# Feed-forward: a second buffer for the activations and a later place for half of the units' sums and splits; mixer: the convolution norm's two sums later

## The chip, the cores and the metric

The kernel runs on one core of one Trainium2 chip. The metric is device time in microseconds (us), the median of several executions; one further execution was profiled. The core's engines work side by side, each through its own queue in order, and meet through semaphores: TensorE (PE in the profile) multiplies matrices into PSUM, VectorE (DVE) and ScalarE (ACT) compute on tiles in PSUM and SBUF, GpSimd (POOL) computes on tiles in SBUF, SyncE (SP) issues most DMAs.

## The reference

Two transformer layers and one RWKV-7 layer over 512 tokens of width 1024, all in float32. The change touches the feed-forward, which occurs three times, and the convolution branch of the RWKV layer:

```
def _sq_relu_mlp(x, w_up, w_down):
    return jnp.square(jax.nn.relu(x @ w_up)) @ w_down      # 1024 -> 4096 -> 1024
...
x = _layer_norm(DN_ALPHA * x + _sq_relu_mlp(x, w_up[i], w_down[i]), ln2_g[i], ln2_b[i])   # layers 0 and 1
...
x = x + jnp.square(jax.nn.relu(h2 @ w_ff1[l])) @ w_ff2[l]                                # RWKV layer
...
def _conformer_conv_mixer(glu_in, conv_w, conv_b, ln_g, ln_b):
    u = glu_in[..., :D_CONV] * jax.nn.sigmoid(glu_in[..., D_CONV:])
    u = causal depthwise convolution of u (31 taps) + conv_b
    u = _layernorm(u, ln_g, ln_b)
    return jax.nn.silu(u)
```

## The kernel before

**Products.** Each float32 operand is split into a rounded part (hi) and the remainder (lo), and a product is three matrix products: hi x hi, hi x lo, lo x hi (`mm3`, lines 290 to 292). A split of a tile in SBUF (`split_sb`, lines 388 and 389) is a copy on ScalarE that makes hi and a subtraction on VectorE or GpSimd that makes lo. Weights come by DMA into `wraw` and are split into `whi` and `wlo`: those of an up unit by `load_w` (lines 265 to 273), those of a down in `down`. There are 6 whi and 6 wlo buffers.

**Feed-forward (`ffn`).** The 4096 hidden features are handled as 16 up units of 256 features. `up(i)` multiplies the weights of a unit with all 512 tokens into two psm tiles (there are two psm buffers; unit 0 uses psa), and ScalarE applies Relu (line 440) and Square (line 441) into the tile `hf`. Two consecutive up units form one of 8 down units. A down is a matrix product of 2 x 2 blocks (token halves and feature halves) done with seven block products instead of eight, so it needs sums and differences of blocks of the activations and of the weights. Those of the activations are the combinations in lines 448 to 451 on VectorE, which write the blocks 3 to 6 of `hf`; the blocks 0 to 2 and then 3 to 6 are split into `hh` and `hl`. Those of the weights are in lines 488 to 493 on GpSimd. The products of a down go into psa tiles, of which there are four, two for each block product, and VectorE adds each to the output x (line 460; line 458 the first time) or to a running sum q (line 505); then the psa tile is free.

The order of issue is up(0), up(1), and then for each down unit u but the last: up(2u + 2), down(u), up(2u + 3). On each engine instructions run in the order of a schedule that was made when the program was built: the order of issue gives the priority, and an instruction that is not ready in the planned time lets others pass. So TensorE's period is: two up units, one down. The first two up units' products are followed by unit 2's, which needs a psm tile back from unit 1's Relu. The buffers of `hh` and `hl` are three deep, `hf` has one.

**Mixer.** In the RWKV layer `second_mixer` works through 8 chunks of 128 features in a software pipeline of stages; in each stage `interleave` mixes several generators: projections, the inverse and the chunk recurrence of earlier chunks, the convolution and the gates. Each generator yields the cost of what it has just issued, has a planned total, and the one with the smallest fraction done is advanced; at a tie the one that stands first in the list. The sums of the convolution's layer norm are one such generator, in stage 7:

```
interleave(*late, *work[::-1], (n, branches(i)))
...
def mean(self):
    ps = self.g.ps("psd")
    self.g.nc.tensor.matmul(ps, self.g.ones, self.sum, start=True, stop=True)
```

`mean` sums over features with a product by ones in a psd tile; `center(j)` loads a chunk, subtracts the mean on GpSimd, stores it, squares it on ScalarE and adds the square on GpSimd to `cnsq`; `var` is a second product by ones in a psd tile, followed by a root on ScalarE and a reciprocal on VectorE. `norm(j)` normalises chunk j in stage 8 and writes it over the rows of H that the gates read; `project` multiplies the result. psd has one buffer; the gates (`branch_gate`, 24 products and a Tanh in line 1318) use it too, two of them in stage 7 and four in stage 8.

Of the kernel before, what the change touches and what calls it, by code (L numbers as in the profile page):

```python
# [11 lines left out]
F32 = mybir.dt.float32  # L12
# [276 lines left out]
def mm3(nc, ps, w, x, first, last):  # L289
    nc.tensor.matmul(ps, w[0], x[0], start=first, stop=False)  # L290
    nc.tensor.matmul(ps, w[0], x[1], start=False, stop=False)  # L291
    nc.tensor.matmul(ps, w[1], x[0], start=False, stop=last)  # L292


def proj_fm(g, W, X, m0, tag="psm"):

    ps = g.ps(tag)
    n = len(W)
    for kc in range(n):
        w = tuple(a[:, m0:m0 + 128] for a in W[kc])  # L300
        mm3(g.nc, ps, w, (X[0][:, kc, :], X[1][:, kc, :]), kc == 0, kc == n - 1)
    return ps
# [84 lines left out]
def split_sb(g, src, hi, lo, eng=None):  # L387
    g.nc.scalar.activation(hi, src, AF.Copy)  # L388
    (eng or g.nc.gpsimd).tensor_tensor(lo, src, hi.bitcast(F32), op=ALU.subtract)  # L389
# [13 lines left out]
def ffn(g, w_up, w_down, X, alpha, hp, tmp, late, norm, fm=None, fill=None):  # L403
# [15 lines left out]
    def first_two(W):  # L419

        pss = [g.ps("psa") for _ in range(2)]
        for half, t in enumerate(HALF_TOKENS):
            for e, ps in enumerate(pss):
                for kc in range(8):
                    w = tuple(a[:, e * 128:e * 128 + 128] for a in W[kc])
                    mm3(nc, ps[:, t], w, (X[0][:, kc, t], X[1][:, kc, t]), kc == 0, kc == 7)
                if half == 0:
                    late[e]()
        return pss

    def up(i):

        plain = i // 2 == units - 1
        W = g.load_w(w_up[:, i * 256:i * 256 + 256], eng=nc.gpsimd if i > 1 else None)
        F = tmp.tile([128, 8, 256], F32, name="hf", tag="hf")
        pss = first_two(W) if i == 0 else None
        for e in range(2):
            p3 = (pss[e] if pss else proj_fm(g, W, X, e * 128)).rearrange("p (a t) -> p a t", a=2)
            o = F[:, 1:3, :] if e else F[:, 0:8:7, :]
            nc.scalar.activation(o, p3, AF.Relu)  # L440
            nc.scalar.activation(o, o, AF.Square)
        hh = hp.tile([128, 7, 256], F32R, name="hh", tag="hh")
        hl = hp.tile([128, 7, 256], F32R, name="hl", tag="hl")
        split_sb(g, F[:, 0:3, :], hh[:, 0:3, :], hl[:, 0:3, :], V)
        if plain:
            split_sb(g, F[:, 7, :], hh[:, 3, :], hl[:, 3, :], V)
        else:
            V.tensor_tensor(F[:, 3, :], F[:, 7, :], F[:, 2, :], op=ALU.add)
            V.tensor_tensor(F[:, 4, :], F[:, 3, :], F[:, 0, :], op=ALU.subtract)
            V.tensor_tensor(F[:, 5, :], F[:, 0, :], F[:, 7, :], op=ALU.subtract)  # L450
            V.tensor_tensor(F[:, 6, :], F[:, 1, :], F[:, 4, :], op=ALU.subtract)  # L451
            split_sb(g, F[:, 3:7, :], hh[:, 3:7, :], hl[:, 3:7, :], V)
        h.append((hh, hl))

    def add(tb, c, ps):
        xs = g.x[tb][:, c * 512:c * 512 + 512]
        if (tb, c) not in seen and alpha != 1.0:
            V.scalar_tensor_tensor(xs, xs, alpha, ps, op0=ALU.mult, op1=ALU.add)
        else:
            V.tensor_tensor(xs, ps, xs, op=ALU.add)  # L460
        seen.add((tb, c))

    def down(u):
        q = w_down[u * 512:u * 512 + 512, :].rearrange("(j e p) n -> e p j n", e=2, p=128)
        new = lambda: g.wraw.tile([128, 1024], F32, name="wraw", tag="wraw")

        def quarter(e, c):
            t = new()
            nc.sync.dma_start(t.rearrange("p (j n) -> p j n", j=2), q[e][:, :, c * 512:c * 512 + 512])
            return t  # L470

        def parts(t, eng=None):
            hi = g.whi.tile([128, 1024], F32R, name="whi", tag="whi")
            lo = g.wlo.tile([128, 1024], F32R, name="wlo", tag="wlo")
            split_sb(g, t, hi, lo, eng)
            return hi, lo

        def product(W, k, ps, first=True, last=True):
            for t in range(2):
                for j in range(2):  # L480
                    x = tuple(a[:, k, t * 128:t * 128 + 128] for a in h[2 * u + j])
                    w = tuple(a[:, j * 512:j * 512 + 512] for a in W)
                    mm3(nc, ps[t], x, w, first and j == 0, last and j == 1)

        b11, b21, b12, b22 = quarter(0, 0), quarter(1, 0), quarter(0, 1), quarter(1, 1)
        B11, B21 = parts(b11), parts(b21)
        t3 = new()
        nc.gpsimd.tensor_tensor(t3, b22, b12, op=ALU.subtract)
        nc.gpsimd.tensor_tensor(b12, b12, b11, op=ALU.subtract)
        nc.gpsimd.tensor_tensor(b11, b22, b12, op=ALU.subtract)  # L490
        T2, T1, T3 = parts(b11), parts(b12, V), parts(t3, V)
        B22 = parts(b22, V)
        nc.gpsimd.tensor_tensor(b21, b21, b11, op=ALU.subtract)
        T4 = parts(b21)

        for k, W in ((1, B11), (2, B21), (6, T2), (5, T1), (7, T3), (3, B22), (4, T4)):
            ps = Q1 if k == 1 else [g.ps("psa") for _ in range(2)]
            product(W, BLOCK[k], ps, k > 1 or u == 0, k > 1 or u == units - 2)
            for t in range(2):
                if k in QS:  # L500
                    q = QS[k][:, t, :]
                    if u == 0:
                        nc.scalar.copy(q, ps[t])
                    else:
                        V.tensor_tensor(q, q, ps[t], op=ALU.add)
                elif k > 1:
                    add(2 * (k == 4) + t, int(k == 3), ps[t])

    def combine(ts):

        for t in ts:
            q5, q6, q7 = (QS[k][:, t, :] for k in (5, 6, 7))
            add(t, 0, Q1[t])
            V.tensor_tensor(q6, q6, Q1[t], op=ALU.add)
            V.tensor_tensor(q7, q7, q6, op=ALU.add)
            V.tensor_tensor(q6, q6, q5, op=ALU.add)
            V.tensor_tensor(q5, q5, q7, op=ALU.add)
            add(t, 1, q6)
            add(2 + t, 0, q7)
            add(2 + t, 1, q5)  # L520

    def down_last(u):
        for c in range(2):
            W = g.load_w(w_down[u * 512:u * 512 + 512, c * 512:c * 512 + 512], eng=nc.gpsimd)
            for tb in range(4):
                ps = g.ps("psa")
                for kc in range(4):
                    k = (kc % 2, 3 - kc % 2)[tb // 2]
                    x = tuple(a[:, k, tb % 2 * 128:tb % 2 * 128 + 128] for a in h[2 * u + kc // 2])
                    mm3(nc, ps, x, W[kc], kc == 0, kc == 3)  # L530
                add(tb, c, ps)
                if (c, tb) == (0, 1):
                    combine((1,))
                if c == 1:
                    norm(tb)
                    if fm and tb > 1:
                        fm(tb - 2)

    up(0)
    up(1)  # L540
    for u in range(units - 1):
        up(2 * u + 2)
        down(u)
        if u == units - 2:
            combine((0,))
        up(2 * u + 3)
    down_last(units - 1)
    if fill:
        fill()
# [575 lines left out]
def second_mixer(g, outer):  # L1125
    nc, tc, d = g.nc, g.tc, g.d
    H = g.X
    with ExitStack() as st:
# [25 lines left out]
        with ExitStack() as s2, ExitStack() as s3, ExitStack() as s4:  # L1154
# [22 lines left out]
            outs = iter(range(8))  # L1177

            def sums():
                yield 0.0  # L1180
                cn.mean()
                yield 4.0
                for j in range(8):
                    cn.center(j, ka)
                    yield 1.0
                cn.var()

            def conv_out(n):
# [52 lines left out]
            for i in range(1, 9):  # L1241
                n = 6.0 * CONVS[i] + 4.0 * GATES[i] + (i == 8) * (8.0 + 4.0 * OUTS[0])
                work = [(16.0, wkv_proj(g, i, parts[i], env))] if i < 8 else []
                work += [(4.0, wkv_inputs(g, i - 1, parts[i - 1], env))]
                late = [(10.0, wkv_inverse(g, i - 2, parts[i - 2], env))] if i > 1 else []
                late += [(17.0, wkv_chunks(g, i - 3, parts[i - 3], env))] if i > 2 else []
                if i == SUMS:
                    work += [(12.7, sums())]
                interleave(*late, *work[::-1], (n, branches(i)))
            s4.close()  # L1250
            cn.pool = g.pool(s4, "wkc", 4, side="right")
# [16 lines left out]
            for m in range(8):  # L1268
                t, u = cn.tile(), cn.tile()
# [488 lines left out]
```

## Time and profile before

| | us |
|---|---|
| median of 3 runs | 2481.47 (2478.55 to 2486.14) |
| profiled execution | 2481.95 |
| its span in the profile | 2479.8 |
| TensorE busy | 2364.9 |

The span runs from the first to the last instruction; the rest of the profiled execution's time lies around it. A time in the profile is a start in us from the span's start. Busy time of TensorE counts matrix products, whose ends are modelled; two starts are a better measure of pace than one duration.

### The profile page before, as it was taken

To read this page: it belongs to the slowest core of one execution; us is meant where nothing else is said; L and a number is where in the kernel's file an instruction comes from. 1 tells how busy PE (TensorE), PEld (TensorE's weight loads), DVE (VectorE), ACT (ScalarE), POOL (GpSimd) and SP (SyncE) were. 2 spreads that over 40 slices of the span, in tenths; PEclk is the share of its full clock that TensorE was granted. 3 is DMA by queue.
4 is the path that set the end of the run, shared out by engine and by line. 5 is a ranking of instruction groups with operands and counts; after the bars stand their busy time and mean duration, and the time that the engine had idled before them with its cause. 6 is when DMAs were issued, how large, how long until landed. Compare 5 with 4: busy or idle time off the path is not lost.

```text
span 2479.8 us, 36415 instructions
## 1 busy us (share of the span) xinstructions
PE 2364.9 (95%) x14140; PEld 1898.6 (77%) x14140; DVE 1481.9 (60%) x2782; ACT 1283.0 (52%) x2005; POOL 1030.6 (42%) x571
## 2 busy tenths in 40 slices
PE   8999999999999999999999999999988999899998
PEld 6779778787777787877777877777766679787786
DVE  3776565666443655564685587877756542645556
ACT  5774454445465645444455454666655533544443
POOL 1114677662111025767632232323253114476772
PEclk9999999999999999999999999999998999999999
DMA  7445232347565244232372576666664468232322
GB/s 209 94 141 166 85 116 71 115 121 172 140 136 117 62 124 121 71 119 86 103 202 85 118 167 146 147 144 150 134 173 119 124 172 248 77 102 85 119 81 73
DMA packets 302349, 312.19 MB, mean 126 GB/s; under 512 B 61280, under 2 KB 234976, under 8 KB 302048
## 3 DMA queue, kind: packets, MB, share of 16 engines
q1 hardware_dynamic: 280432, 239.60, 31.9%
q0 software_dynamic: 21168, 68.17, 15.2%
q8 instruction: 111, 1.82, 0.3%
q10 hardware_dynamic: 576, 2.10, 0.2%
q14 instruction: 62, 0.51, 0.1%
HBM read 221.47 MB, written 20.19 MB: 97 GB/s over the span
## 4 chain that ended last, share of the span: by engine, by line
PE 55%; POOL 13%; issue 11%; DVE 9%; DMA 6%; ACT 6%; SPq 0%; POOLq 0%; DVEq 0%; ACTq 0%
PE psm L290 7%; PE psm L291 7%; PE psm L292 7%; POOL wlo L389 4%; PE psa L290 4%; PE psa L291 4%; PE psa L292 4%; POOL wlo L273 3%; DMA wlo<-wraw 2%; PE pst L1416 2%; PE psd L290 2%; PE pss L292 2%; PE pss L291 2%; PE pss L290 2%; PE psd L292 2%
## 5 line engine op out<-in xcount | busy, mean ns | idle before, releaser
L290 PE MATMUL psm<-xT,whi 128*128 128x512 f32 (+1 forms) x1192 | 476.2, 400 | 23.3 <-ACT hf L440 12.3
L292 PE MATMUL psm<-xT,wlo 128*128 128x512 f32 (+1 forms) x1192 | 469.7, 394 | 5.4 <-DMA wlo<-wraw 5.4
L291 PE MATMUL psm<-xT,whi 128*128 128x512 f32 (+1 forms) x1192 | 471.0, 395 | 0.5 <-DVE xT L352 0.5
L267 ACT ACTIVATE whi<-wraw 128x1024 fp32r<-128x1024 f32 (+3 forms) x287 | 285.7, 1005 | 290.8 <-PE psa L292 101.5
L271 POOL DMA_DIRECT2D wlo<-wraw x147 | 127.3, 872 | 729.0 <-ACT wlo L270 497.4
L273 POOL TENSOR_TENSOR wlo<-wraw,whi 128x1024 fp32r<-128x1024 f32 x122 | 315.5, 2620 | 102.0 <-ACT whi L267 73.4
L389 POOL TENSOR_TENSOR wlo<-wraw,whi 128x1024 fp32r<-128x1024 f32 x84 | 212.9, 2534 | 241.9 <-ACT whi L388 241.9
L290 PEld LDWEIGHTS psm<-xT,whi 128*128 128x128 f32 x1192 | 226.7, 190 | 74.7 <-ACT hf L440 13.6
L292 PEld LDWEIGHTS psm<-xT,wlo 128*128 128x128 f32 x1192 | 226.6, 190 | 53.1 <-DMA wlo<-wraw 6.5
L291 PEld LDWEIGHTS psm<-xT,whi 128*128 128x128 f32 x1192 | 227.4, 191 | 44.6 <-DVE xT L352 0.9
L290 PE MATMUL psa<-whi,hh 128*128 128x512 f32 x600 | 239.0, 398 | 15.6 <-DVE x L460 15.5
L291 PE MATMUL psa<-wlo,hh 128*128 128x512 f32 x600 | 236.6, 395 | 0.0
L292 PE MATMUL psa<-whi,hl 128*128 128x512 f32 x600 | 236.4, 395 | 0.0
L388 ACT ACTIVATE whi<-wraw 128x1024 fp32r<-128x1024 f32 x147 | 151.7, 1053 | 123.9 <-PE psa L292 61.8
L1407 DVE SCALAR_TENSOR_TENSOR psc<-glu,cw,psc 128x512 f32<-128x512 f32 x232 | 173.8, 749 | 5.9 <-ACT psc L1403 2.2
L388 ACT ACTIVATE hh<-hf 128x768 fp32r<-128x768 f32 (+1 forms) x96 | 87.8, 914 | 145.2 <-DVE hf L451 143.4
L389 DVE TENSOR_TENSOR hl<-hf,hh 128x768 fp32r<-128x768 f32 (+1 forms) x96 | 124.3, 1295 | 60.2 <-ACT hh L388 60.2
L290 PEld LDWEIGHTS psa<-whi,hh 128*128 128x128 f32 x600 | 112.8, 188 | 49.7 <-DVE x L460 23.1
L389 DVE TENSOR_TENSOR wlo<-wraw,whi 128x1024 fp32r<-128x1024 f32 x63 | 86.4, 1396 | 92.5 <-ACT whi L388 87.8
L270 ACT ACTIVATE wlo<-whi 128x1024 fp32r<-128x1024 f32 (+3 forms) x147 | 140.1, 956 | 2.3 <-PE psm L292 0.7
L292 PEld LDWEIGHTS psa<-whi,hl 128*128 128x128 f32 x600 | 112.8, 188 | 27.2 <-DVE hl L389 0.7
L291 PEld LDWEIGHTS psa<-wlo,hh 128*128 128x128 f32 x600 | 112.8, 188 | 25.8
(464 smaller groups left out, 5208.6 us busy)
## 6 DMA issues: line engine op xcount, KB each, us to landing
wlo<-wraw POOLq DMA_DIRECT2D x123, 512.0 KB, 5.3
wraw<-in_w_up SPq DMA_DIRECT2D x64, 512.0 KB, 4.5
wraw<-in_w_down SPq DMA_DIRECT2D x64, 512.0 KB, 3.6
wraw<-in_w_ff SPq DMA_DIRECT2D x64, 512.0 KB, 3.8
wraw<-in_w_in SPq DMA_DIRECT2D x56, 512.0 KB, 4.9
wraw<-in_od_w_in SPq DMA_DIRECT2D x24, 512.0 KB, 4.3
wraw<-in_ple_w_gate SPq DMA_DIRECT2D x16, 512.0 KB, 4.6
brow<-in_rows SPq DMA_DIRECT2D x13, 512.0 KB, 6.7
```

Source lines behind the costliest of these rows:

```text
L267: nc.scalar.activation(hi[:, :m], raw[:, :m], AF.Copy)
L270: nc.scalar.activation(lo[:, :m], hi[:, :m].bitcast(F32), AF.Copy, scale=-1.0)
L271: nc.gpsimd.dma_start(lo[:, :m].bitcast(F32), raw[:, :m], accum_op=ALU.add)
L273: eng.tensor_tensor(lo[:, :m], raw[:, :m], hi[:, :m].bitcast(F32), op=ALU.subtract)
L290: nc.tensor.matmul(ps, w[0], x[0], start=first, stop=False)
L291: nc.tensor.matmul(ps, w[0], x[1], start=False, stop=False)
L292: nc.tensor.matmul(ps, w[1], x[0], start=False, stop=last)
L388: g.nc.scalar.activation(hi, src, AF.Copy)
L389: (eng or g.nc.gpsimd).tensor_tensor(lo, src, hi.bitcast(F32), op=ALU.subtract)
L1407: nc.vector.scalar_tensor_tensor(acc if j == 30 else part, u[:, j:j + 512], cw[:, fc * 31 + j:fc * 31 + j + 1], part, op0=ALU.mult, op1=AL ...
L1416: nc.tensor.matmul(ps[o], lhs[o], rhs[o], start=start, stop=stop)
```

## The change

In the feed-forward `hf` gets a second buffer, and `up` ends behind Relu and Square; what it did with `hf` after that (combinations and splits) becomes the function `blocks`, which `up` returns with its arguments bound. For units 0, 1 and 2u + 3 it is called at once, as before; for the units 2u + 2 it is called behind down(u). In the mixer the generator `sums` yields 2 parts instead of 0 ahead of the mean and 3 further parts ahead of the variance, and its planned total goes from 12.7 to 17.5.

```
--- before.py
+++ after.py
@@ -432,13 +432,16 @@
 
         plain = i // 2 == units - 1
         W = g.load_w(w_up[:, i * 256:i * 256 + 256], eng=nc.gpsimd if i > 1 else None)
-        F = tmp.tile([128, 8, 256], F32, name="hf", tag="hf")
+        F = tmp.tile([128, 8, 256], F32, name="hf", tag="hf", bufs=2)
         pss = first_two(W) if i == 0 else None
         for e in range(2):
             p3 = (pss[e] if pss else proj_fm(g, W, X, e * 128)).rearrange("p (a t) -> p a t", a=2)
             o = F[:, 1:3, :] if e else F[:, 0:8:7, :]
             nc.scalar.activation(o, p3, AF.Relu)
             nc.scalar.activation(o, o, AF.Square)
+        return functools.partial(blocks, F, plain)
+
+    def blocks(F, plain):
         hh = hp.tile([128, 7, 256], F32R, name="hh", tag="hh")
         hl = hp.tile([128, 7, 256], F32R, name="hl", tag="hl")
         split_sb(g, F[:, 0:3, :], hh[:, 0:3, :], hl[:, 0:3, :], V)
@@ -536,14 +539,16 @@
                     if fm and tb > 1:
                         fm(tb - 2)
 
-    up(0)
-    up(1)
+    up(0)()
+    up(1)()
     for u in range(units - 1):
-        up(2 * u + 2)
+
+        later = up(2 * u + 2)
         down(u)
+        later()
         if u == units - 2:
             combine((0,))
-        up(2 * u + 3)
+        up(2 * u + 3)()
     down_last(units - 1)
     if fill:
         fill()
@@ -1177,12 +1182,13 @@
             outs = iter(range(8))
 
             def sums():
-                yield 0.0
+                yield 2.0
                 cn.mean()
                 yield 4.0
                 for j in range(8):
                     cn.center(j, ka)
                     yield 1.0
+                yield 3.0
                 cn.var()
 
             def conv_out(n):
@@ -1245,7 +1251,7 @@
                 late = [(10.0, wkv_inverse(g, i - 2, parts[i - 2], env))] if i > 1 else []
                 late += [(17.0, wkv_chunks(g, i - 3, parts[i - 3], env))] if i > 2 else []
                 if i == SUMS:
-                    work += [(12.7, sums())]
+                    work += [(17.5, sums())]
                 interleave(*late, *work[::-1], (n, branches(i)))
             s4.close()
             cn.pool = g.pool(s4, "wkc", 4, side="right")
```

## Rows read from the trace of the kernel before

**Rows 1.** The page: busy time, share of the span and instructions of each engine.
```profile
PE 2364.9 (95%) x14140; PEld 1898.6 (77%) x14140; DVE 1481.9 (60%) x2782; ACT 1283.0 (52%) x2005; POOL 1030.6 (42%) x571
```

**Rows 2.** Who waited for whom: us in total, times, longest us.
```profile
PE psa L290 <- DVE x L460: 15.5, 14, 1.7
PE psm L290 <- ACT hf L440: 12.3, 3, 4.7
...
PE psq L1661 <- DVE s L1655: 4.3, 3, 2.7
PE psd L1368 <- POOL cnsq L1363: 4.1, 1, 4.1
...
PE psd L1350 <- POOL cnsum L1345: 1.8, 1, 1.8
...
ACT hf L440 <- DVE hl L389: 27.3, 20, 1.6
```

**Rows 3.** Timeline of TensorE, feed-forward: start us, us, instruction, [idle before <-releaser].
```profile
361.64 0.39 PE L292 MATMUL psa<-whi,hl 128*128 128x512 f32 x1
363.18 0.50 PE L290 MATMUL psa<-whi,hh 128*128 128x512 f32 x1 [1.14 <-DVE x L460]
363.51 0.39 PE L291 MATMUL psa<-wlo,hh 128*128 128x512 f32 x1
...
449.39 0.50 PE L290 MATMUL psa<-whi,hh 128*128 128x512 f32 x1 [1.69 <-DVE x L460]
```

**Rows 4.** Timeline of VectorE, the same period.
```profile
357.08 0.42 DVE L448 TENSOR_TENSOR hf<-hf 128x256 f32<-128x256 f32 x1
...
360.30 2.22 DVE L389 TENSOR_TENSOR hl<-hf,hh 128x1024 fp32r<-128x1024 f32 x1 [0.53 <-ACT hh L388]
362.44 0.68 DVE L460 TENSOR_TENSOR x<-psa,x 128x512 f32<-128x512 f32 x1
...
369.06 0.69 DVE L460 TENSOR_TENSOR x<-psa,x 128x512 f32<-128x512 f32 x1 [0.70 <-PE psa L292]
```

**Rows 5.** Timeline of ScalarE, the same period.
```profile
350.14 1.06 ACT L388 ACTIVATE hh<-hf 128x1024 fp32r<-128x1024 f32 x1 [5.69 <-DVE hf L451]
352.56 0.60 ACT L440 ACTIVATE hf<-psm 128x512 f32<-128x512 f32 x1 [1.35 <-DVE hl L389]
...
359.20 1.06 ACT L388 ACTIVATE hh<-hf 128x1024 fp32r<-128x1024 f32 x1 [0.51 <-DVE hf L451]
```

**Rows 6.** Timeline of GpSimd, the same period.
```profile
358.77 2.66 POOL L389 TENSOR_TENSOR wlo<-wraw,whi 128x1024 fp32r<-128x1024 f32 x1 [10.15 <-ACT whi L388]
361.40 10.47 POOL L273 TENSOR_TENSOR wlo<-wraw,whi 128x1024 fp32r<-128x1024 f32 x4
```

**Rows 7.** Instructions on the tile hf: ns of one, minimum/median/maximum.
```profile
L389 DVE TENSOR_TENSOR hl<-hf,hh x96: 416/959/3159, 247.0 to 2450.8; 128x768 fp32r<-128x768 f32 x48, 128x1024 fp32r<-128x1024 f32 x42, 128x256 fp32r<-128x256 f32 x6
...
L448 DVE TENSOR_TENSOR hf<-hf x42: 410/847/2632, 243.2 to 2408.9; 128x256 f32<-128x256 f32 x42
```

**Rows 8.** Timeline of ScalarE at the first entry of a feed-forward.
```profile
252.66 1.06 ACT L388 ACTIVATE hh<-hf 128x1024 fp32r<-128x1024 f32 x1 [8.57 <-DVE hf L451]
255.07 0.60 ACT L440 ACTIVATE hf<-psm 128x512 f32<-128x512 f32 x1 [1.35 <-DVE hl L389]
```

**Rows 9.** Windows behind two entries: stretch, us, TensorE busy (products), granted clock, DMA.
```profile
255.70:259.40 3.70, 3.68 (x9) 0.54 0.02 4
...
2148.70:2154.00 5.30, 5.21 (x13) 0.53 0.03 6
```

**Rows 10.** Timeline of the mixer: the two sums; a gate's Tanh, first and last of six.
```profile
1803.69 1.12 PE L1350 MATMUL psd<-cnsum,ca 128*128 128x512 f32 x2 [1.81 <-POOL cnsum L1345]
...
1860.96 2.07 PE L1368 MATMUL psd<-cnsq,ca 128*128 128x512 f32 x2 [4.10 <-POOL cnsq L1363]
...
1833.14 0.69 ACT L1318 ACTIVATE bgt<-psd,half 128x512 f32<-128x512 f32 x1
...
1922.73 0.69 ACT L1318 ACTIVATE bgt<-psd,half 128x512 f32<-128x512 f32 x1
```

More of the change, by code (lines that the diff above doesn't have):

```diff
@@ L434, in up @@
         W = g.load_w(w_up[:, i * 256:i * 256 + 256], eng=nc.gpsimd if i > 1 else None)
-        F = tmp.tile([128, 8, 256], F32, name="hf", tag="hf")
+        F = tmp.tile([128, 8, 256], F32, name="hf", tag="hf", bufs=2)
         pss = first_two(W) if i == 0 else None
@@ L441, in up, with blocks @@
             nc.scalar.activation(o, o, AF.Square)
+        return functools.partial(blocks, F, plain)
+    def blocks(F, plain):
         hh = hp.tile([128, 7, 256], F32R, name="hh", tag="hh")
@@ L537, in down_last @@
                         fm(tb - 2)
-    up(0)
-    up(1)
+    up(0)()
+    up(1)()
     for u in range(units - 1):
-        up(2 * u + 2)
+        later = up(2 * u + 2)
         down(u)
+        later()
         if u == units - 2:
             combine((0,))
-        up(2 * u + 3)
+        up(2 * u + 3)()
     down_last(units - 1)
@@ L1179, in sums @@
             def sums():
-                yield 0.0
+                yield 2.0
                 cn.mean()
@@ L1185, in sums @@
                     yield 1.0
+                yield 3.0
                 cn.var()
@@ L1247, in second_mixer @@
                 if i == SUMS:
-                    work += [(12.7, sums())]
+                    work += [(17.5, sums())]
                 interleave(*late, *work[::-1], (n, branches(i)))
```

## The prediction

> **What bounds the kernel now.** I read the page first: TensorE is busy 95% of the span [rows 1]. So a change can only win what TensorE idles, 115 us in all, or make it idle more. Next the list of who waited for whom, which says which of these idle times the change touches. Four entries do [rows 2]: TensorE waits 15.5 us in 14 places for an accumulation that frees a psa buffer (L460), 12.3 us in 3 places for a Relu that frees a psm buffer (L440), and 4.1 us and 1.8 us once each for the mixer's two sums. Together 33.7 us, 1.4% of the time. Then the timeline of one feed-forward period, engine by engine, for the reason of the first entry; the entry of a feed-forward for the second; the mixer's timeline for the last two.
>
> The wait at 363.18 recurs two periods later at 449.39, so a period (two up units of 48 products each, one down of 84) takes 43 us [rows 3]. Until 361.64 products start 0.23 us apart; the next starts 1.54 us later, and the one after that 0.33 us later. So an idle time of 1.14 us costs 1.31 + 0.10 = 1.41 us. It waits for the accumulation at 362.44, whose products had ended well before: VectorE was in the 2.22 us split of the unit's last four blocks, which began at 360.30 [rows 4]. Follow that split back: it needs the copy hh at 359.20 on ScalarE, this the combinations from 357.08 on, these the unit's Relu, which started at 352.56 [rows 4, 5]. And that Relu had waited 1.35 us for "DVE hl L389": not for its products, but until the unit before had been read out of the only hf buffer. This wait stands 20 times in the list, 27.3 us in all [rows 2]. So a late Relu makes a late split, a late split a late accumulation, and this the idle TensorE.
>
> **The change, part by part.**
>
> *The second hf buffer.* It costs no instruction. The Relu at 352.56 no longer waits for hl. What is late next is ScalarE itself: ahead of the Relu in its queue stands the copy hh of the unit before (350.14 to 351.20), which had waited 5.69 us for VectorE's combinations [rows 5]. I leave that order as it is: a combination takes 0.41 us at least and 2.63 at most [rows 7], and in an order planned with the small figure the copy is ready before the Relu's products are. So the chain starts 1.35 us earlier, and all of it moves: Relu, Square, copies, split, accumulation. The longest of the 14 waits are 1.69 and 1.70 us [rows 2, 3], the other twelve together 12.1 us, so 1.0 us each: these vanish, and of the two some 0.4 us each stays. In lost time: 15.5 + 14 x 0.27 (the restart, 1.41 - 1.14) = 19.3 us, less 1 us that stays: 18 us. Bounds: nothing, if another wait ends last at the same moment; 19.3 us.
>
> *The held-back sums and splits.* For 21 of the 48 units two copies hh, up to four combinations and two splits are issued behind the down products of the unit before: none added, none removed. They are needed one down later, after a further 48 products (11 us), so being late costs them nothing. What they can cost is VectorE's order. The down's products last 43 - 1.4 - 96 x 0.227 = 19.8 us; in them stand 12 accumulations of 0.69 us (8.3 us) and two weight splits; the held work that remains is, unhindered, three combinations of 0.42 us, a split of 0.96 and one of 4/3 of that: 3.5 us [rows 4, 7]. There is room for all. If the accumulations go first, they are in time; if VectorE takes the held work whenever it has nothing else, the order stays what it is and the 1.35 us decides. I take nothing extra for this part. Bounds: 0 and the price of the third rival.
>
> This price depends on GpSimd. The same combination takes 0.41 to 2.63 us, the same kind of split 0.96 at the median and 3.16 at most; an accumulation, which reads one operand from PSUM, took 0.69 us at 369.06 in the middle of 10.47 us of GpSimd work [rows 4, 6, 7]. The Trainium skill ("GPSIMD Engine Reference", Key points) says that GpSimd shares its SBUF interfaces with VectorE, in contention with VectorE instructions that have two SBUF inputs; these rows agree, and by that rule the change is the wrong way round, since it puts two-input work where GpSimd is busiest: that is the third rival's time. By the rows alone GpSimd rests for 10.15 us until 358.77 [rows 6], and the held work, ready some 1.35 us before its 357.08, still begins ahead of that.
>
> *The entry of a feed-forward.* Three times TensorE stops for the Relu of unit 1, 12.3 us [rows 2]. The first of these Relus started at 255.07, right behind the copy hh (252.66 to 253.72) and 1.35 us more for the one hf buffer [rows 8]. Behind such a wait the granted clock is 0.54 for 3.7 us, the lower of the two levels (1.2 of 2.4 GHz): 9 products in 3.68 us, which at 0.227 take 2.04, a loss of 1.6 us; at the third entry 0.53 for 5.3 us, 13 products, 2.3 us lost [rows 9]. With 1.6 us for the second as well the entries cost 12.3 + 5.5 = 17.8 us. If the copy stays ahead of the Relu, 1.35 us is won at each, 4 us together, and the lower clock still follows. If the Relu goes first on ScalarE, all is won. The copy had waited 8.57 us for slowed combinations [rows 8]; an order planned without that slowness keeps it first. I take 4 us, bounds 0 and 17.8.
>
> *The mixer's sums.* The mean's product waits for the last addition on GpSimd, the variance's too [rows 10]. Both are issued later now. psd has one buffer, and the stage's first gate is now issued ahead of the mean: it holds psd until its Tanh, which was at 1833.14. So the mean moves not by the 2 of 17.5 parts that the code names, but by some 28 us, to about 1832. All behind it moves too: eight loads, subtractions, stores, squares and additions on the SP queue, GpSimd and ScalarE. From mean to variance it took 57 us (1803.69 to 1860.96), so the variance comes near 1889, inside the next stage. Its normalisations write over the rows that the gates read, so they can't finish before the last gate's Tanh at 1922.73 anyway [rows 10]: 33 us of cover for the root, the reciprocal and the first few normalisations, while TensorE has gates and chunks to do. Gone: 1.8 + 4.1 = 5.9 us. Perhaps gone too: a wait of 2.7 us for VectorE's short operations [rows 2], which run beside the sums' GpSimd work now; but the same work then meets others, and I set these against each other. I take 5 us. Bounds: 11 us lost (second rival); 5.9 + 2.7 = 8.6 us won.
>
> **The sum.** 18 + 4 + 5 = 27 us. The profiled execution took 2481.95 us (span 2479.8 and 2.15 around it), 0.5 us over the median of 2481.47. 2481.95 - 27 = 2455 us, 1.1% faster.
>
> **The rivals.**
>
> First: the Relu of unit 1 goes ahead of the copy at the entries. Then 18 + 17.8 + 5 = 40.8, so 2441 us. For it: the copy is ready much later than the Relu. Against: it is ready first in any order that counts combinations at 0.42 us.
>
> Second: the mixer pays. The variance needs psd as well, and can miss its turn between two gates: from 1833.14 to 1922.73 six gates end, 18 us apart [rows 10]. Then it slips past 1905, the normalisations miss the last gate, and the projections behind them, which fill TensorE between short dependent products, come late. With two gates' worth of filler missing (2 x 24 x 0.227 = 11 us): 2481.95 - 22 + 11 = 2471 us. For it: one psd buffer for three users. Against: the 33 us of cover.
>
> Third, on the other side: the held work lands among the accumulations while GpSimd works (358.77 to 371.87 [rows 6]). Hindered it is 3 x 2.63 + 3.16 + 2.22 = 13.3 us instead of 3.5. One such operation between two accumulations, which come 1.4 us apart, pushes the queue back by 0.69 + 2.6 - 1.4 = 1.9 us. The accumulation that ran at 362.44 is ready near 358 and needed at 361.64: 3 us beside its own 0.69. From the second such operation on TensorE stops, from the third for longer than now. Three: 5.7 - 3 = 2.7 us instead of 1.4 in each of 18 periods, 23 us more, with 9 us won elsewhere: 2496 us. All five: 9.5 - 3 = 6.5 us, 5.1 more in each: 2481.95 + 92 - 9 = 2565 us. Against: the held work is ready before the accumulations are.
>
> Fourth: in the steady periods the buffer does nothing, because the split's copy waits for something that didn't move. Then 4 to 9 us are won: 2473 to 2478 us. For it: ScalarE's queue also carries the weight copies. Against: the 1.35 us stands right before the Relu, and nothing else.
>
> **How the numbers follow.** Forecast 0.55, first 0.11, second 0.17, third 0.07, fourth 0.10. The forecast's own range is 2447 to 2463. The range 2438 to 2478 leaves out the third rival and the far ends of the first, second and fourth, about 2 in 10. 0.3% is 7.4 us, about what a measurement of this kernel can tell from no change, so 2474 and 2489 are the borders. Faster: forecast 0.55, first 0.11, most of the second (0.13), some of the fourth (0.04): 0.83. Same: 0.04 + 0.06 = 0.10. Slower: 0.07.
>
> **What would show it.** "psa L290 <- DVE x L460" falls from 15.5 us to under 3; "ACT hf L440 <- DVE hl L389" is gone; a period takes 41.5 us. "psm L290 <- ACT hf L440" stays, near 8 us, with the low clock behind it; gone, it is the first rival. The mean's product stands behind a gate's Tanh, without a wait, near 1817 (28 us later, less what two feed-forwards won before). I am wrong if splits of 2 us and more stand between accumulations, or if the projections start further behind the last gate than now.

## The result, and the profile after

The changed kernel took 2454.68 us (median, 2451.57 to 2456.77), the kernel before 2482.09 beside it: a ratio of 0.9888, 95% interval 0.9869 to 0.9907. The forecast was 2455. The profiled execution took 2454.41 us, its span is 2452.6; all rows of "after" below are from it.

First the page of the changed kernel: the engines' busy time, and the group of the down units' first products (line, engine, operation, tiles, forms, count; busy us and mean ns of one; idle us ahead of it).

```profile
PE 2354.9 (96%) x14140; PEld 1898.8 (77%) x14140; DVE 1479.0 (60%) x2782; ACT 1284.6 (52%) x2005; POOL 1029.1 (42%) x571
...
L290 PE MATMUL psa<-whi,hh 128*128 128x512 f32 x600 | 237.4, 396 | 0.1
```

Then who waited for whom in the changed kernel (us in total, times, longest).

```profile
PE psm L290 <- DVE ksl L758: 9.0, 2, 5.4
PE psm L290 <- ACT hf L440: 8.6, 3, 3.8
...
PE psd L1374 <- POOL cnsq L1369: 3.8, 1, 3.8
PE psq L1422 <- DVE st L1681: 3.3, 4, 2.6
...
PE psq L1667 <- DVE s L1661: 2.5, 3, 1.7
```

No instruction came or went [rows 1]. The 15.5 us for the accumulation [rows 2] are gone: the products into psa now stand 0.1 us idle in the whole span. "ACT hf L440 <- DVE hl L389", 27.3 us before, isn't in the list, whose smallest entry is 2.1 us. The Relu at the entries still costs 8.6 us. Of the mixer's two sums the mean has left the list and the variance has not.

Now the period of the first feed-forward that [rows 3 to 5] showed of before, in TensorE's timeline: the first psa product of this down, the three around the place where the wait was, and the first of the next down.

```profile
351.00 0.39 PE L290 MATMUL psa<-whi,hh 128*128 128x512 f32 x1
...
357.74 0.40 PE L292 MATMUL psa<-whi,hl 128*128 128x512 f32 x1
357.97 0.41 PE L290 MATMUL psa<-whi,hh 128*128 128x512 f32 x1
358.21 0.40 PE L291 MATMUL psa<-wlo,hh 128*128 128x512 f32 x1
...
392.29 0.39 PE L290 MATMUL psa<-whi,hh 128*128 128x512 f32 x1
```

VectorE in the same stretch:

```profile
351.47 0.42 DVE L451 TENSOR_TENSOR hf<-hf 128x256 f32<-128x256 f32 x1
...
354.68 2.24 DVE L389 TENSOR_TENSOR hl<-hf,hh 128x1024 fp32r<-128x1024 f32 x1 [0.53 <-ACT hh L388]
356.84 0.68 DVE L463 TENSOR_TENSOR x<-psa,x 128x512 f32<-128x512 f32 x1
```

and ScalarE:

```profile
346.00 1.06 ACT L388 ACTIVATE hh<-hf 128x1024 fp32r<-128x1024 f32 x1 [5.61 <-DVE hf L454]
346.97 0.58 ACT L440 ACTIVATE hf<-psm 128x512 f32<-128x512 f32 x1
...
353.59 1.06 ACT L388 ACTIVATE hh<-hf 128x1024 fp32r<-128x1024 f32 x1 [0.51 <-DVE hf L454]
```

The Relu now follows the copy hh of the unit before at once, without the 1.35 us for hl. In before this down's first psa product stood at 354.91, so all of [rows 3 to 5] may be laid 3.91 us earlier: the split that began at 360.30 would be at 356.39 and is at 354.68, 1.71 us sooner. It is as long as ever (2.24 us) and still stands ahead of the accumulation, which ends at 357.52. The product that needs the tile starts at 357.97, in step with its neighbours. So the wait is gone by 0.45 us, not by much. From one down to the next it is 41.29 us, where 41.5 was forecast. The 43 read of before lie between two places with different waits; from one down's first product to the next down's (354.91 to 397.61) it was 42.70, so a period is 1.41 us shorter: the wait of 1.14 us with its restart.

### The profile page after: what moved, and what is told of

It reads as the page before. It is cut to its first block, busy times and chain, and to the rows that moved or that the text cites. A ratio compares the mean times of both kernels' runs of the same rounds, so it can differ in the third digit from the quotient of the medians.

```text
span 2452.6 us, 36343 instructions
## 1 busy us (share of the span) xinstructions
PE 2354.9 (96%) x14140; PEld 1898.8 (77%) x14140; DVE 1479.0 (60%) x2782; ACT 1284.6 (52%) x2005; POOL 1029.1 (42%) x571
## 4 chain that ended last, share of the span: by engine, by line
PE 71%; ACT 6%; DMA 6%; issue 6%; POOL 5%; DVE 5%; SPq 0%; POOLq 0%; DVEq 0%; ACTq 0%
PE psm L290 10%; PE psm L292 10%; PE psm L291 10%; PE psa L290 6%; PE psa L291 6%; PE psa L292 6%; DMA wlo<-wraw 3%; PE pst L1422 2%; PE psd L290 2%; PE pss L292 2%; PE pss L291 2%; PE pss L290 2%; PE psd L292 2%; PE psd L291 2%; POOL wlo L389 1%
## 5 line engine op out<-in xcount | busy, mean ns | idle before, releaser
L290 PE MATMUL psm<-xT,whi 128*128 128x512 f32 (+1 forms) x1192 | 476.0, 400 | 23.0 <-DVE ksl L758 9.0
L389 POOL TENSOR_TENSOR wlo<-wraw,whi 128x1024 fp32r<-128x1024 f32 x84 | 217.5, 2589 | 209.7 <-ACT whi L388 209.7
L290 PEld LDWEIGHTS psm<-xT,whi 128*128 128x128 f32 x1192 | 226.6, 190 | 73.7 <-issue 11.1
L290 PE MATMUL psa<-whi,hh 128*128 128x512 f32 x600 | 237.4, 396 | 0.1
L389 DVE TENSOR_TENSOR hl<-hf,hh 128x768 fp32r<-128x768 f32 (+1 forms) x96 | 124.3, 1295 | 58.0 <-ACT hh L388 57.9
L389 DVE TENSOR_TENSOR wlo<-wraw,whi 128x1024 fp32r<-128x1024 f32 x63 | 93.6, 1509 | 86.6 <-ACT whi L388 72.2
L290 PEld LDWEIGHTS psa<-whi,hh 128*128 128x128 f32 x600 | 112.9, 188 | 27.9 <-ACT hh L388 0.9
L292 PEld LDWEIGHTS psa<-whi,hl 128*128 128x128 f32 x600 | 112.9, 188 | 27.2 <-DVE hl L389 0.7
```

## The experiments

All ratios are to the kernel before on the same chip. FFN time below is worked out from each profile: from the first to the last Relu of a feed-forward, summed over the three. It is 950.5 us before and 923.1 after.

**The buffer alone.** The kernel before, with one edit:

```
-        F = tmp.tile([128, 8, 256], F32, name="hf", tag="hf")
+        F = tmp.tile([128, 8, 256], F32, name="hf", tag="hf", bufs=2)
```

> The kernel before with the second hf buffer alone: nothing is held back, the mixer is as before. Theory A (the one hf buffer makes the Relu late, and the late split blocks the accumulation): the 14 waits for the accumulation (15.5 us) go, the three entry waits fall from 12.3 to about 8.6 us; 22 to 27 us faster than before, so 2455 to 2460 us. Rival B (it is the issue order: the held-back splits let the accumulations pass): the 14 waits stay, only the entries win, 2474 to 2478 us.

Measured: 2457.9 us, 0.9894 [0.9875, 0.9912]; FFN 931.5 us. Its waits:

```profile
PE psm L290 <- ACT hf L440: 9.4, 3, 3.6
...
PE psd L1368 <- POOL cnsq L1363: 3.9, 1, 3.9
```

The psa wait falls to 0.4 us in one place and the Relu's wait for hl is gone here too, with nothing held back. From the first to the last Relu of each feed-forward every engine's instructions stand in the same order as in the kernel before: the buffer moved none of them, it took a wait away.

**The held-back sums and splits alone.** `blocks` and `later()` as in the change, but `hf` with its one buffer and the mixer as before.

> The kernel before with the splits held back behind the down products, but with one hf buffer; the mixer as before. Theory A: the Relu still waits for the buffer, the waits for the accumulation stay (over 10 us in all), and the time is that of before within 5 us, 2478 to 2487 us. Rival B: the waits are gone without the buffer, 2460 to 2466 us.

Measured: 2483.7 us, 0.9999 [0.9987, 1.0011]; FFN 951.5 us. Its waits:

```profile
ACT hf L440 <- DVE hl L389: 26.0, 19, 1.6
PE psa L290 <- DVE x L463: 14.5, 15, 1.7
```

Both stand almost as in [rows 2]. The reason is plain from the two traces: on every engine the instructions stand in the same order as in the kernel before, with the same shapes and the same semaphores, over the whole span. `later()` moves a call in the source, and in the schedule built from it no instruction has moved. So this run is the kernel before once more, and it took the same time.

**Both edits of the feed-forward**, the mixer as before.

> The changed feed-forward (second hf buffer and held-back splits) with the mixer of before. Theory A (holding back adds nothing once there are two buffers): as the second buffer alone, a ratio of 0.987 to 0.992 to before, so 2462 to 2473 us where before takes 2485. Rival B (holding back wins some us of its own, since the three feed-forwards of the changed kernel's profile are 8 us shorter than those of the second buffer alone): 0.984 to 0.987.

Measured: 2460.71 us, 0.9904 [0.9891, 0.9917]; FFN 927.8 us. Beside 0.9894 for the buffer alone, holding back adds nothing to the buffer either, and again the order on every engine is that of the run without it (but for two neighbours on VectorE, which start within 0.01 us of each other).

**The mixer's sums alone** (the change's `yield 2.0`, `yield 3.0` and 17.5, the feed-forward as before).

> The kernel before with the later sums in the mixer alone. Theory A on the mixer (the mean behind the first gate takes GpSimd's work off VectorE's short recurrence, and the mean's wait goes; the variance's wait of 4 us stays): 5 to 8 us faster than before, 2474 to 2477 us. Rival (the mixer's gain in the changed kernel is only a shift against the work around it and is lost again): within 3 us of before, 2479 to 2485 us.

Measured: 2477.02 us, 0.9964 [0.9951, 0.9976], 9 us. The variance's wait of 4 us, which was expected to stay, isn't in this profile.

**The mean later, nothing else:**

```
-                yield 0.0
+                yield 2.0
                 cn.mean()
...
-                    work += [(12.7, sums())]
+                    work += [(14.5, sums())]
```

> The kernel before with the mean 2 parts later and nothing else: the 3 further parts ahead of the variance are left out, the planned total is 14.5. Theory (the mixer's gain is the mean's new place behind the first gate alone): as with both moves, 0.995 to 0.998 of before. Rival (the variance's later place matters): half of that or less, 0.998 to 1.001.

Measured: 2476.99 us, 0.9969 [0.9958, 0.998], 8 us. On every engine its instructions stand in the same order as in the run before it (but for two pairs of neighbours, which start within 0.05 us of each other), so the three parts ahead of the variance move nothing: the mean, once behind a gate, takes the variance along.

**No sums on GpSimd.** The kernel before, with 15 of the 16 GpSimd operations between mean and variance left out: all eight subtractions and seven of the eight copies and additions of squares (the text below says 14). The normalisation isn't computed.

> The kernel before, with 14 of the 16 GpSimd operations between mean and variance left out (all eight subtractions of the mean and six of the eight additions of squares; one addition stays so that the variance's product has an operand), so the normalisation is not computed. Theory (in the stage of the sums GpSimd slows VectorE's short recurrence, and TensorE waits for it and falls to the lower clock): the recurrence at that place takes 8 to 9 us instead of 13 to 14, the variance's wait of 4 us goes too, and the time falls by 8 to 14 us, 0.994 to 0.997 of before. Rival (the recurrence is slow for another reason): only the variance's wait goes, 3 to 5 us, 0.998 to 0.999.

Measured: 2471.21 us, 0.995 [0.9937, 0.9963], 12 us. This run shows what the forecast had left at zero. In the kernel before, VectorE's timeline holds a recurrence of 30 short operations (`mbt`, `mb`) beside the sums:

```profile
1819.79 0.20 DVE L1566 TENSOR_TENSOR mbt<-mb,ub 64x48 f32<-64x48 f32 x1
...
1820.11 1.17 DVE L1568 TENSOR_TENSOR mb<-mb,mbt 64x48 f32<-64x48 f32 x1
1821.32 1.23 DVE L1566 TENSOR_TENSOR mbt<-mb,ub 64x55 f32<-64x55 f32 x1
1822.57 1.18 DVE L1568 TENSOR_TENSOR mb<-mb,mbt 64x55 f32<-64x55 f32 x1
...
1824.61 1.30 DVE L1568 TENSOR_TENSOR mb<-mb,mbt 64x63 f32<-64x63 f32 x1
...
1826.69 1.17 DVE L1568 TENSOR_TENSOR mb<-mb,mbt 64x63 f32<-64x63 f32 x1
```

and GpSimd's timeline of the kernel before in the same 8 us:

```profile
1819.94 1.27 POOL L1363 TENSOR_TENSOR cnsq<-cnsq,cn 128x512 f32<-128x512 f32 x1 [2.33 <-ACT cn L1359]
1821.17 1.30 POOL L1546 TENSOR_TENSOR ka<-ka,cb 128x512 f32<-128x512 f32 x1
1822.42 1.26 POOL L1363 TENSOR_TENSOR cnsq<-cnsq,cn 128x512 f32<-128x512 f32 x1
...
1824.56 1.27 POOL L1357 TENSOR_TENSOR cn<-cn,cnsum 128x512 f32<-128x512 f32 x1 [0.88 <-DMA cn<-cod]
1826.46 1.33 POOL L1357 TENSOR_TENSOR cn<-cn,cnsum 128x512 f32<-128x512 f32 x1 [0.62 <-DMA cn<-cod]
```

Each short operation that begins inside a GpSimd operation lasts until that one ends (1820.11 + 1.17 = 1821.28, against 1819.94 + 1.27 = 1821.21), 1.2 us instead of 0.2, five times. TensorE waits twice for VectorE meanwhile:

```profile
1824.25 0.33 PE L1416 MATMUL psq<-vtk,ka 64*64 64x64 f32 x4 [1.85 <-DVE st L1675]
...
1828.05 0.69 PE L1661 MATMUL psq<-s,md 128*128 128x64 f32 x2 [2.69 <-DVE s L1655]
```

The second is the prediction's wait of 2.7 us. With the sums' operations left out only one of the 30 is slow, again beside a GpSimd operation, and the recurrence takes 8.8 us instead of 13.8. TensorE's products stand in the order of the kernel before until well past this place. Counted from the Tanh of the gate ahead of the first one of [rows 10] (1789.53 before, 1792.12 here), the 251st product starts 28.46 us later in both runs, at the start of the recurrence, and the 337th 44.24 us later before and 38.49 here: 5.8 us sooner, with nothing reordered on TensorE. The Trainium skill ("GPSIMD Engine Reference", Key points) says that the two engines contend for their SBUF interfaces where a VectorE instruction has two SBUF inputs; these rows agree, and they add that a stall ends with the GpSimd operation.

**The buffer and the later mean, nothing else.**

> The kernel before with only two edits: the second hf buffer, and two parts ahead of the mean (total 14.5). Nothing is held back and the variance has no further parts. Theory (these two edits are the whole change): a ratio to before as the changed kernel had it, 0.9885 to 0.9888, so 0.987 to 0.990, about 2456 us; the wait of psa for x stays under 1 us. Rival (the held-back sums or the variance's parts carry a share once both halves are there): 0.991 or more, 2462 us or more, with the psa waits back or VectorE's short recurrence slowed again.

Measured: 2454.15 us, 0.9861 [0.9838, 0.9884]; the changed kernel on the same chip (below) 2453.41. The ratio is a little under the expected 0.987, but the order on every engine is that of the changed kernel, semaphores included: these two edits are the whole change.

**The Relu of unit 1 ahead of the copy hh.** The changed kernel, but units 0 and 1 are both multiplied and activated before their sums and splits are issued, and the order of unit 0's split of the blocks 3 to 6, which begins with the copy hh, is set behind unit 1's first Relu (`behind[0]`):

```
-    up(0)()
-    up(1)()
+    first, second = up(0), up(1)
+    first()
+    second()
...
+                with g.tc.issue_after(behind[0]):
+                    split_sb(g, F[:, 3:7, :], hh[:, 3:7, :], hl[:, 3:7, :], V)
```

> The changed kernel, but at the entry of each feed-forward ScalarE's second copy hh of unit 0 is queued behind the first Relu of unit 1. Theory: what is left of the entry wait (8.6 us in three places, and 1.2 us of half clock behind the third) is this queue order alone: the wait goes, 9 to 10 us faster than the changed kernel, 2444 to 2446 us. Rival: another wait takes its place (the weights of unit 2, or the splits of units 0 and 1, which now end later for the first down): 0 to 4 us faster, 2451 to 2455 us.

Measured: 2445.05 us, 0.9832 [0.9812, 0.9853]; FFN 915.9 us. Its four times lay 12 us apart, so it ran once more:

> The run in which the Relu of unit 1 goes ahead of the copy hh, once more, in more rounds: its four times lay 12 us apart. Theory (the waits of the three entries go and the low clock behind them with them, in every execution): 0.983 to 0.985, 9 to 14 us under the changed kernel, and no product at half pace at any of the three entries. Rival (only the waits of 8.6 us are won for good; that no low clock followed was chance in that execution): 0.985 to 0.986, with a low clock at one entry or another.

Measured: 2439.83 us, 0.9813 [0.9799, 0.9828]; FFN 912.9 us, better than the expected ratio. ScalarE in this run at the first entry:

```profile
246.59 0.60 ACT L441 ACTIVATE hf<-psm 128x512 f32<-128x512 f32 x1 [2.27 <-PE psm L292]
253.03 1.06 ACT L388 ACTIVATE hh<-hf 128x1024 fp32r<-128x1024 f32 x1 [5.84 <-DVE hf L457]
253.99 0.62 ACT L444 ACTIVATE hf<-hf 128x512 f32<-128x512 f32 x1
```

The Relu waits for its products alone and stands 6.44 us ahead of the copy. What is left of "PE psm L290 <- ACT hf" is 0.4 us in the one run and 0.6 in the other, at the third entry. Beside the changed kernel on the same chip it wins 13.6 us (2453.41 - 2439.83). It is faster than both kernels, and is the version to keep.

**The changed kernel twice more.**

> The changed kernel once more, beside the other runs on this chip. If the parts add up (second buffer 0.9894, mixer alone 0.9964), its ratio to before is 0.984 to 0.988; if the mixer's gain is partly lost behind the faster feed-forward, it is 0.988 to 0.991 as in its first comparison.

Measured: 2456.43 us, 0.9885 [0.987, 0.9899]; FFN 928.4 us.

> The changed kernel on the same chip beside the other two, as their measure: 0.987 to 0.990. Theory (the clock behind the same wait differs between executions): waits of about 3 us at the entries as before, and a number of products at half pace behind each that differs from the three profiles so far (0, 0 and 9 of some; 5, 13 and 6). Rival (the clock follows the wait's length): the same lengths give the same number of slow products as in the profile of the changed kernel.

Measured: 2453.41 us, 0.9868 [0.9851, 0.9885]; FFN 924.2 us. The buffer's 0.9894 times the mixer's 0.9964 would be 0.9858; the four ratios measured for this program (0.9888, 0.9885, 0.9868 and, without the parts that move nothing, 0.9861) lie on it or up to 0.003 above. What the profiles of one and the same kernel say of the clock stands in the last section.

## Why the prediction was right, point by point

**The steady periods: right, and for the reason given.** 18 us were forecast. The psa waits fell from 15.5 us to nothing; with the restart of 0.27 us at each of 14 that is 19.3 us, the upper bound of that term. The two longest waits, of which some 0.4 us each was to stay, went as well: the chain moved by 1.71 us, not 1.35, since the copy ahead of the Relu also came some 0.2 us sooner against the down. The fourth rival (the buffer does nothing here) falls with the buffer alone. All kernels with one hf buffer have FFN times of 950.5 to 953.2 us (five profiles), all with two and the entry untouched 923.1 to 931.5 (six): 951.7 - 926.8 = 24.9 us on the mean, against 22 forecast for periods and entries together.

**The held-back work: rightly nothing, because nothing was held back.** Three pairs agree: alone 0.9999; with the buffer 0.9904 against 0.9894; in the whole change 2453.41 against 2454.15 without it. Of the two cases in the prediction it is the second, "the order stays what it is", and more strictly than meant: in each pair the order on every engine is the same. So the room on VectorE and the third rival (held work among the accumulations beside GpSimd) were never put to the test; that the rival didn't come (0.0 to 0.4 us of idle ahead of the psa products in all three profiles of the changed kernel) says nothing about what held work would cost there. Why the schedule puts these instructions in the same places isn't shown. One sign that I had named was a wrong one: "splits of 2 us and more" do stand ahead of accumulations still, at 354.68, and cost nothing while they end in time.

**The entries: the wait right, the clock mis-sized.** 4 us were forecast: 1.35 us at each of three. The wait fell from 12.3 to 8.6 us, 3.7. That the order would stay was right (the Relu stands behind the copy, and the first rival wasn't realised), and what the rival was worth was nearly right once the order was made by hand: 13.6 us more, where the forecast's 17.8 less 4 is 13.8. That closeness is partly luck: between the profiles of the changed kernel's third run and of this one the waits fell by 7.9 us (8.3 were counted) and the products at half pace by some 2.7 us (5.5 were counted); the feed-forwards are 11.3 us apart, and what is missing to 13.6 lies outside them or between executions. What failed is "the lower clock still follows". Windows behind the three entries of the changed kernel (stretch, us, TensorE busy and products, granted clock, DMA):

```profile
254.60:258.30 3.70, 3.67 (x16) 1.00 0.02 4
953.50:957.20 3.70, 3.70 (x16) 1.00 0.02 4
2127.30:2132.60 5.30, 5.28 (x17) 0.73 0.04 7
```

Sixteen products where [rows 9] had nine. At two of the three entries of this profile no low clock followed; the products at half pace cost 1.4 us, against 5.7 us before (both from the distances between starts). So in this execution the entries gave 3.7 + 4.3 = 8 us.

**The mixer: 5 us forecast; 8 to 9 us alone, 4 to 6 us on top of the feed-forward's edits; the reason half wrong.** (0.0036 and 0.0031 of 2485 us are 9 and 8; 0.9904 less 0.9888 is 4; the mean of 0.9904 and 0.9894 less that of the four ratios with the later mean is 6.) The sums in TensorE's and two gates' Tanh in ScalarE's timeline of the changed kernel:

```profile
1810.93 1.10 PE L1356 MATMUL psd<-cnsum,ca 128*128 128x512 f32 x2 [0.40 <-ACT bgt L1324]
...
1859.77 2.08 PE L1374 MATMUL psd<-cnsq,ca 128*128 128x512 f32 x2 [3.82 <-POOL cnsq L1369]
...
1810.10 0.69 ACT L1324 ACTIVATE bgt<-psd,half 128x512 f32<-128x512 f32 x1
...
1899.20 0.67 ACT L1324 ACTIVATE bgt<-psd,half 128x512 f32<-128x512 f32 x1
```

The mean stands right behind a gate's Tanh, as forecast, with a wait of 0.40 us, at 1810.93 (1817 forecast). Measured from the start of the recurrence (1818.50 before, 1802.51 after) it moved by 23 us, not 28; the variance moved by 15. "Gone: 1.8 + 4.1" failed in its larger half. The mean's wait is gone in all eight profiles with the later mean. The wait of 4.1 us for the last addition is 3.8 us here, 4.0 in the third run of the same kernel and 3.0 in the second run of the Relu's edit; in the other five, the second run of the changed kernel among them, there is none. And it is worth nothing that shows: from the Tanh ahead of this stage (1789.53 before, 1775.71 here) to the next feed-forward's first Relu it is 334.3 to 335.6 us in the three with the wait and 332.0 to 335.3 in the five without. A gain came instead from the term that I had "set against" another at nothing: the recurrence no longer runs beside the sums. In this kernel one of its 30 operations is slow, and it takes 8.8 us:

```profile
1802.51 0.85 DVE L1572 TENSOR_TENSOR mbt<-mb,ub 64x15 f32<-64x15 f32 x1 [0.63 <-DMA ub<-ud]
1803.39 0.17 DVE L1574 TENSOR_TENSOR mb<-mb,mbt 64x15 f32<-64x15 f32 x1
```

and the GpSimd operation that the slow one began in:

```profile
1802.04 1.30 POOL L1552 TENSOR_TENSOR ka<-ka,cb 128x512 f32<-128x512 f32 x1 [7.78 <-ACT ka L1551]
```

In all kernels with the early mean it takes 12.7 to 14.1 us with five slow operations (four profiles), in all with the later mean or without the sums 8.1 to 8.8 with none or one (nine). How TensorE is filled there, in three windows of 44 us from that Tanh (columns as above), first of before:

```profile
1789.50:1833.50 44.00, 37.45 (x336) 0.92 0.66 166
```

and of after:

```profile
1775.70:1819.70 44.00, 42.70 (x394) 1.00 0.62 145
```

and of the run without the sums on GpSimd, whose products stand in the order of before:

```profile
1792.10:1836.10 44.00, 41.04 (x382) 1.00 0.73 190
```

The 6.55 us of idle before are the mean's wait of 1.81 us and waits of 0.20, 1.85 and 2.69 for VectorE; without the sums' operations 3.6 of them go, and with the later mean 5.25, the mean's wait with them. All kernels with the early mean have 37.5 to 38.2 us of busy time in this window (four profiles), all with the later one 42.7 to 42.8 (eight). Behind it the work meets other waits: over the whole stretch to the next feed-forward TensorE's waits for VectorE's `st` and `s` add up to 5.2 to 11.0 us with the early mean and 5.6 to 11.4 with the later one, so there the two did cancel, as forecast. The stretch takes 336.1 to 342.4 us with the early mean and 332.0 to 335.6 with the later, 5.9 on the mean. That the 5 us came out is thus partly luck, and which waits make up the whole of the 8 to 9 us isn't separated.

The second rival (the variance misses its turn, the normalisations the last gate) didn't come: the last gate's Tanh went from 1922.73 to 1899.20, 23.5 us sooner. The sign named for it, projections further behind the last gate, shows a little: from that Tanh to the next feed-forward's first Relu it is 211.1 us, 208.1 before (2130.84 - 1922.73). In all profiles it is 206.6 to 210.9 us with the early mean (four) and 209.1 to 211.3 with the later one (eight), so some 1.5 us of the gain are given back.

**The sum.** 27 us were forecast; the profiled executions are 27.5 us apart, their spans 27.2. The parts of these two profiles are not the forecast's: 27.4 us won in the feed-forwards (22 forecast), 3.9 in the stretch from the second to the third of them with the RWKV mixer (5), and 4.0 lost between the first two (389.3 to 393.3 us), where nothing was edited. In the two further profiles of the changed kernel that last stretch took 388.8 and 393.3 us, so it differs between executions. So does the stretch with the mixer: 864.6 and 870.5 us in the two runs with the buffer and the early mean, 863.5 to 867.5 in the four with the buffer and the later one. That the total was met so closely is partly luck: what the entries' clock gave beyond the forecast, this stretch took.

## What to carry to other kernels

Follow an idle time back until a wait appears that is for a buffer and not for data: here 15 us of an engine's waits for an accumulation hung on a Relu, four steps earlier, that waited for its tile to be read out, and one more buffer, without any reordering, took all of them. Before an order is changed by hand, check with one part alone whether the buffer doesn't do it; and where a late instruction stands ahead of an early one on the same queue because the plan counted it at its undisturbed time, set the order yourself (13.6 us here, half of what the whole change won). Before an edit is timed, compare the order of the instructions on each engine: two parts of this change, the held-back work and the variance's three parts, moved none. And a chain of short VectorE operations is better kept away from long GpSimd ones: TensorE got through the same products 5.8 us sooner where this chain was left alone.

## What the runs showed of the hardware that wasn't expected

**The clock behind the same wait differs between executions.** Before, the low clock stood behind each entry, and I took it as given. The windows of the changed kernel's third run at the same entries as above:

```profile
254.00:257.70 3.70, 3.70 (x16) 1.00 0.02 4
952.70:956.40 3.70, 3.65 (x16) 1.00 0.02 4
2123.90:2129.20 5.30, 5.30 (x13) 0.50 0.04 10
```

and of its second run:

```profile
254.40:258.10 3.70, 3.70 (x10) 0.58 0.02 4
951.00:954.70 3.70, 3.70 (x9) 0.50 0.02 4
2124.90:2130.20 5.30, 5.30 (x17) 0.71 0.04 9
```

The waits ahead of the first entry were 2.89, 2.79 and 2.75 us in the three profiles of this kernel, and 0, 0 and 7 products behind them ran at half pace (1.2 of 2.4 GHz). At the third entry the first and the third profile have almost the same wait, 3.78 and 3.81 us, and 6 and 13 such products. Over the eleven profiles with these waits: behind the four of 1.89 and 1.90 us none did; behind the eight of 2.7 to 3.04 us none in two and 6 to 14 in six; behind all twenty-one of 3.35 us and more, 6 to 14. A wait of 3 us is thus worth 3 to 6 us. Which it is differs between executions of one kernel; what decides it, no run here shows. Only the version without the wait (0.4 and 0.6 us at the third entry, none at the others) showed no slow product in either of its runs.

**A VectorE operation of 0.2 us with two inputs in SBUF that begins inside such an operation on GpSimd lasts until that one ends.** It holds for every one of the recurrence's operations in all thirteen profiles and all chunks: the 187 that began inside a GpSimd addition, subtraction or product ended 0.03 to 0.08 us behind it. The 104 that began while GpSimd was issuing a DMA took their 0.16 to 0.21 us. The stall isn't a factor on its own duration: 64x48 and 64x63 elements took 1.17 and 1.30 us alike, the rest of one 1.27 us GpSimd operation. So this chain paid the rest of one GpSimd operation per meeting, up to 1.3 us.
